# The softmax reciprocal of a windowed attention: 256 wide on VectorE, or four wide with a copy on GpSimd

## The chip, the cores and the metric

One core of one Trainium2 chip runs the whole program. The time is device microseconds of one execution, and the figure of a kernel is the median of its runs. The engines are named as the profile names them: PE is TensorE's matmul queue and PEld its weight loads, DVE is VectorE, ACT is ScalarE, POOL is GpSimd and SP issues the DMAs.

## The reference, cut to what matters

The program is one inference step of a two-layer decoder trunk: a pooling layer, then a layer of sliding-window attention, each followed by a convolutional feed-forward block and a gate. Prompt rows (1024) and sampled rows (8 sequences of 4) pass together. The change touches the attention of the prompt rows:

```python
s = einsum('nbqhgd,nbjhd->nbhgqj', q, k) * (HEAD_DIM ** -0.5)
s = where(valid, s + bias, -inf)
m = maximum(max(s, axis=-1, keepdims=True), sink)
e = exp(s - m)
p = e / (sum(e, axis=-1, keepdims=True) + exp(sink - m))
o = einsum('nbhgqj,nbjhd->nbqhgd', p, v)
```

There are 16 query heads of 64 values in four groups of four, one K/V head for each group, blocks of 128 queries, and 256 keys (the block before and the block itself) for each.

## The kernel before, in words

The matmul stages around the attention are one long stream of products in which each fp32 operand is split into a high and a low part (`xh` and `xl` for the activations, `wh` and `wl` for the weights, helper `split`, L140 and L141; products at L157 and L163 to L165). The attention stands in the middle, at about 1.1 to 1.33 ms.

The attention's work is cut into 32 items `(p, t, r)`: `p` is a pair of K/V heads (2), `t` a block of 128 queries (8), `r` one head of the pair (2). An item has four query heads, its index `g` within the tiles. Two items with the same `p` and `t` make a pair, which share an output bank. For an item, in order:

- `prep` (L919 to L930) splits the queries: the high half `qs` by ACT (r = 1, L925) or DVE (r = 0, L927), a copy of it into the other half by POOL (L928), and the low part `qz` by POOL (L929).
- `scores` (L932 to L949), in two halves of two heads: PE multiplies into one of two PSUM banks (L944, L945), and DVE adds the bias and takes the row maximum (L948).
- `peak` (L954, DVE) makes the negative maximum for the exponent, and `rest` (L958, DVE) the exponent of the sink.
- `exps` (L964 and L966, ACT) takes the exponentials; each gives its row sum into `sm[:, 2, g]`.
- `sums` (L970, DVE) adds the sink's term to the four sums.
- `flips` (L976, DVE) takes the reciprocals into the tile `rc`. It reads the four sums through a broadcast over 64 columns and so divides 128 x 256 elements; the 64 equal columns of a head are what the later transpose needs.
- `turn` (L988 to L991), for each half of the keys: PE transposes the exponentials into PSUM, ACT copies them out as the high part (L990), and DVE takes the low part (L991).
- `values` (L1011 to L1013, PE) multiplies them with V into the pair's output bank.
- For a pair: `spread` transposes `rc` (L998, PE) and copies it out (L1000, ACT), `scale` multiplies the output with it (L1017, DVE), and `outs` splits the result into `xh` (L1022, ACT) and `xl` (L1023, POOL).

Items 0 and 1 are begun inside the stream of the query projection, by the helpers `lead` and `soft`, where a planner orders the instructions. From item 2 on the order on every compute engine is the order written out in the loop at L1194 to L1221, under a manual schedule. One step of that loop, for `i`, works on several items at once: sums of item i + 2, `prep` of i + 5, scores of i + 4, exponentials of i + 3, transposes of i + 1, values of i, and at its end `flips` of i + 2 and `rest` of i + 4:

```python
at(i + 2, 2, sums)
at(i + 5, 6, prep)
...
pair(i, spread)
...
at(i + 2, 2, flips)
at(i + 4, 0, rest)
```

The reciprocals of an item are thus taken two steps before `spread` reads them. `rc` has three buffers, `sm` eight. At steps 0 to 8 of each half `p`, the attention of the sampled rows is put in between (`of_sample`), with a small reciprocal of its own at L1073. After the loop comes the output projection (L1286 to L1314), whose weights come by SP's queue into buffers that the attention held.

Of the kernel before, what the change touches and what calls it, by code (L numbers as in the profile page):

```python
# [21 lines left out]
P = 128  # L22
# [64 lines left out]
def trunk(ctx, tc, a, o):  # L87
    nc = tc.nc
    V, A, G, PE = nc.vector, nc.scalar, nc.gpsimd, nc.tensor
# [664 lines left out]
    def attention(es, awp, wv, E, rst):  # L754
# [162 lines left out]
        made = {}  # L917
# [54 lines left out]
        def flips(p, t, r):  # L972
            sm = made[p, t, r][1]
            if r == 0:
                made["rc", p, t] = ap_.tile([P, 4, 2, 64], F32, name="rc", tag="rc", bufs=3)
            V.reciprocal(out=made["rc", p, t][:, :, r, :], in_=sm[:, 2, :].unsqueeze(2).to_broadcast([P, 4, 64]))  # L976

        def turn(p, t, r, kt):

# [145 lines left out]
        def soft(it):  # L1125
            for gp in range(2):
                exps(*it, gp)
            sums(*it)
            flips(*it)
# [42 lines left out]
        with tc.manual_schedule(engines=COMPUTE):  # L1172
# [21 lines left out]
            for i in range(len(items)):  # L1194
                if i == 0:
                    n = q_squares()
                at(i + 2, 2, sums)
                at(i + 5, 6, prep)
                pair(i - 1, scale)
                at(i + 1, 0, turn, 0)  # L1200
                at(i, 0, values, 0)
                at(i + 4, 0, scores, 0)
                at(i + 3, 4, exps, 0)
                at(i + 4, 0, scores, 1)
                at(i + 1, 0, turn, 1)
                pair(i - 1, outs)
                at(i + 4, 0, peak)
                at(i + 3, 4, exps, 1)
                at(i, 0, values, 1)
                pair(i, spread)  # L1210
                p, t, r = items[i]
                step = 2 * t + r - 2
                if step in of_sample:
                    of_sample[step](p)
                at(i + 2, 2, flips)
                at(i + 4, 0, rest)
                if i == 0:
                    squares_sum(*n)
                    root(*n)
                if i == 1:  # L1220
                    scaled(*n)  # L1221
# [150 lines left out]
```

## Time and profile before

| | us |
|---|---|
| median of 3 runs | 2334.55 |
| lowest and highest | 2329.47, 2336.28 |
| the profiled execution | 2332.21 |
| its span in the profile | 2330.4 |

The profiled execution lies 2.34 us under the median; 1.81 us of it lie outside the span. Over the span the profile gives, for each engine, the time in which an instruction of it ran (busy), and for a stretch the TensorE clock that was granted, 1.00 being full speed. The mean of the clock over the span is 0.988. The chain of waits follows the work that ended last back from step to step; its pieces are shorter than the instruction's own duration where the next one on the same engine overlaps it.

### The profile page before, as it was taken

The page shows a single profiled execution, that of the slowest core. Times are in us where ns is not written, and L with a number is a line of the kernel's source. Part 1 is how long each engine was busy: PE and PEld are TensorE (multiplying, and loading weights), DVE is VectorE, ACT ScalarE, POOL GpSimd, SP SyncE. Part 2 cuts the span into 40 slices and gives each one's busy share as a digit, 9 for nine tenths or more (in the row PEclk, how much of TensorE's full clock was granted, in tenths as well). Part 3 has the DMA queues.
Part 4 walks back from the last instruction along what each step waited for, and adds up shares of the span by engine and source line. Part 5 has one row for each costly group of instructions (what it writes and reads, how often), then busy time and mean ns, then how long its engine had stood idle before and what let it go on. Part 6 is the DMA issues. An engine that isn't in the chain of part 4 may idle for free.

```text
span 2330.4 us, 34347 instructions
## 1 busy us (share of the span) xinstructions
PE 2272.7 (98%) x14037; PEld 2219.8 (95%) x14037; DVE 1403.1 (60%) x2122; ACT 822.7 (35%) x1489; POOL 443.6 (19%) x552
## 2 busy tenths in 40 slices
PE   9999999999999999999978899999999999999999
PEld 8999999999999999999866799999999999999898
DVE  5755555555556477567799827645555545555943
ACT  6532222222222244446677615322222222222532
POOL 1420001100001123314445313111000110001300
PEclk7899999999999999999999999999999999999999
DMA  4152211111111122312111141211111111111221
GB/s 137 32 129 87 64 46 46 46 46 46 46 46 46 46 68 75 95 43 49 28 46 28 59 109 55 73 52 46 46 46 46 46 46 46 46 46 47 61 78 43
DMA packets 199264, 133.09 MB, mean 57 GB/s; under 512 B 36355, under 2 KB 183508, under 8 KB 198939
## 3 DMA queue, kind: packets, MB, share of 16 engines
q1 hardware_dynamic: 199107, 130.90, 19.5%
q8 instruction: 110, 1.80, 0.3%
q14 instruction: 47, 0.39, 0.1%
HBM read 117.62 MB, written 18.79 MB: 59 GB/s over the span
## 4 chain that ended last, share of the span: by engine, by line
PE 82%; DVE 13%; ACT 2%; DMA 1%; issue 1%; SPq 1%; POOL 0%; ACTq 0%; DVEq 0%; POOLq 0%
PE mm L157 64%; DVE xl L212 2%; PE ub L163 2%; PE ub L164 2%; PE ub L165 2%; DVE rc L976 2%; PE dps L320 2%; DVE e L948 2%; DVE wl L991 1%; PE qkp L163 1%; PE qkp L165 1%; PE qkp L164 1%; DVE h L634 1%; DVE wl L141 1%; PE aux L163 1%
## 5 line engine op out<-in xcount | busy, mean ns | idle before, releaser
L157 PE MATMUL mm<-xh,wh 128*128 128x352 f32 x2208 | 477.6, 325 | 1.3 <-DVE ext L566 1.3
L157 PE MATMUL mm<-xh,wl 128*128 128x352 f32 x2208 | 476.6, 323 | 0.0
L157 PE MATMUL mm<-xl,wh 128*128 128x352 f32 x2208 | 475.7, 324 | 0.0
L140 ACT ACTIVATE wh<-wr 128x1024 fp32r<-128x1024 f32 x166 | 175.8, 1060 | 740.7 <-PE mm L157 623.3
L157 PEld LDWEIGHTS mm<-xh,wl 128*128 128x128 f32 x2208 | 379.0, 188 | 0.4 <-DVE wl L141 0.2
L157 PEld LDWEIGHTS mm<-xh,wh 128*128 128x128 f32 x2208 | 376.0, 189 | 1.5 <-issue 1.5
L157 PEld LDWEIGHTS mm<-xl,wh 128*128 128x128 f32 x2208 | 374.8, 188 | 0.6 <-issue 0.6
L563 DVE TENSOR_TENSOR ext<-mm,R 128x704 f32<-128x704 f32 x88 | 78.5, 892 | 474.7 <-PE mm L157 466.5
L569 POOL COPY sto<-ext 128x2 f32<-128x2 f32 x88 | 103.7, 1179 | 970.7 <-DVE ext L565 970.7
L624 DVE TENSOR_TENSOR h<-mm,h 128x1056 f32<-128x1056 f32 x160 | 200.9, 1256 | 115.6 <-PE mm L157 115.1
L141 DVE TENSOR_TENSOR wl<-wr,wh 128x1024 fp32r<-128x1024 f32 x164 | 204.9, 1250 | 8.9 <-ACT wh L140 8.9
L157 PE MATMUL mm<-ah,wh 128*128 128x352 f32 x960 | 208.2, 325 | 0.0
L157 PE MATMUL mm<-al,wh 128*128 128x352 f32 x960 | 207.4, 324 | 0.0
L157 PE MATMUL mm<-ah,wl 128*128 128x352 f32 x960 | 206.0, 323 | 0.0
L157 PEld LDWEIGHTS mm<-ah,wl 128*128 128x128 f32 x960 | 163.7, 189 | 0.0
L157 PEld LDWEIGHTS mm<-al,wh 128*128 128x128 f32 x960 | 163.4, 188 | 0.0
L157 PEld LDWEIGHTS mm<-ah,wh 128*128 128x128 f32 x960 | 162.4, 188 | 0.3
L163 PE MATMUL ub<-xh,wh 128*128 128x352 f32 x432 | 142.1, 329 | 0.1
L165 PE MATMUL ub<-xh,wl 128*128 128x352 f32 x432 | 140.2, 325 | 0.0
L164 PE MATMUL ub<-xl,wh 128*128 128x352 f32 x432 | 139.2, 322 | 0.0
L221 POOL TENSOR_TENSOR acc<-acc,sq 128x352 f32<-128x352 f32 x84 | 93.4, 1114 | 197.0 <-ACT sq L220 194.6
L576 DVE SCALAR_TENSOR_TENSOR cg<-ext,cw,cg 128x1072 f32<-128x1072 f32 x88 | 117.4, 1335 | 16.3 <-ACT cg L574 14.9
(275 smaller groups left out, 3634.7 us busy)
## 6 DMA issues: line engine op xcount, KB each, us to landing
wr<-in_w_up_dram SPq DMA_DIRECT2D x88, 512.0 KB
wr<-in_w_down_dram SPq DMA_DIRECT2D x44, 512.0 KB
wr<-in_w_ple_gate_dram SPq DMA_DIRECT2D x16, 512.0 KB
hd<-h SPq DMA_DIRECT2D x8, 528.0 KB
h<-hd SPq DMA_DIRECT2D x8, 528.0 KB
xt<-in_x_prompt_dram SPq DMA_DIRECT2D x8, 512.0 KB
wr<-in_w_q_dram SPq DMA_DIRECT2D x16, 256.0 KB
wr<-in_w_o_dram SPq DMA_DIRECT2D x32, 128.0 KB
```

The costliest lines, as they stand in the source:

```text
L140: A.activation(out=wh, in_=flat, func=AF.Copy)
L141: (low or V).tensor_tensor(out=wl, in0=flat, in1=wh.bitcast(F32), op=ALU.subtract)
L157: PE.matmul(ps[:, c, :C], w[k], b[k][:, c * C:(c + 1) * C], start=st, stop=sp)
L163: PE.matmul(ps, wh[k], bh[k][:, cs], start=k == 0, stop=False)
L164: PE.matmul(ps, wh[k], bl[k][:, cs], start=False, stop=False)
L165: PE.matmul(ps, wl[k], bh[k][:, cs], start=False, stop=k == nk - 1)
L212: V.scalar_tensor_tensor(out=xl[:, m, cs], in0=hm, scalar=gains[:, gain, m:m + 1], in1=xh[:, m, cs].bitcast(F32), op0=ALU.mult, op1=ALU.su ...
L221: G.tensor_tensor(out=st["acc"][:, cs], in0=st["acc"][:, cs], in1=sq, op=ALU.add)
L563: V.tensor_tensor(out=e[:, 2:2 + 2 * C].rearrange("p (c n) -> p c n", n=C), in0=ps[:, 0:2, :C], in1=R[:, :2 * C].rearrange("p (c n) -> p c ...
L569: G.tensor_copy(out=sto[:, j, 0:2], in_=e[:, NP:NP + 2])
L576: V.scalar_tensor_tensor(out=c, in0=e[:, k:k + CO], scalar=cw[:, k, j:j + 1], in1=c, op0=ALU.mult, op1=ALU.add)
L624: V.tensor_tensor(out=three(f.h[:, m, :]), in0=ps[:, :, :C], in1=three(f.h[:, m, :]), op=ALU.add)
```

## The change

```diff
         def flips(p, t, r):
             sm = made[p, t, r][1]
             if r == 0:
                 made["rc", p, t] = ap_.tile([P, 4, 2, 64], F32, name="rc", tag="rc", bufs=3)
-            V.reciprocal(out=made["rc", p, t][:, :, r, :], in_=sm[:, 2, :].unsqueeze(2).to_broadcast([P, 4, 64]))
+            V.reciprocal(out=sm[:, 3, :], in_=sm[:, 2, :])
+            G.tensor_copy(out=made["rc", p, t][:, :, r, :], in_=sm[:, 3, :].unsqueeze(2).to_broadcast([P, 4, 64]))
```

VectorE (`V`) takes four reciprocals in each partition into the fourth row of `sm`, which nothing used; GpSimd (`G`) copies them into `rc` through the same broadcast over 64 columns. `flips` stands at the same place of the written order.

## Rows read from the trace of the kernel before

**Rows 1.** The page, parts 1 and 4: busy time per engine, chain by line.

```profile
...
PE 2272.7 (98%) x14037; PEld 2219.8 (95%) x14037; DVE 1403.1 (60%) x2122; ACT 822.7 (35%) x1489; POOL 443.6 (19%) x552
...
PE mm L157 64%; DVE xl L212 2%; PE ub L163 2%; PE ub L164 2%; PE ub L165 2%; DVE rc L976 2%; PE dps L320 2%; DVE e L948 2%; DVE wl L991 1%; PE qkp L163 1%; PE qkp L165 1%; PE qkp L164 1%; DVE h L634 1%; DVE wl L141 1%; PE aux L163 1%
...
```

**Rows 2.** Windows: us; busy of PE, PEld, DVE, ACT, POOL (instructions); clock; DMA.

```profile
...
1130.00:1155.00 25.00, 23.82 (x151) 23.29 (x151) 18.40 (x45) 17.58 (x48) 6.63 (x7) 1.00 0.08 22
1173.43:1184.99 11.56, 8.82 (x45) 7.50 (x43) 9.73 (x24) 7.80 (x22) 3.16 (x3) 0.78 0.01 2
1184.99:1320.20 135.21, 108.86 (x710) 87.01 (x710) 132.90 (x425) 107.85 (x352) 68.81 (x97) 0.97 0.12 40
1320.20:1328.74 8.54, 6.60 (x37) 5.17 (x38) 8.54 (x11) 6.55 (x14) 2.58 (x2) 1.00 0.00 1
...
```

**Rows 3.** Chain of waits in one steady pair of heads: start us, us, what.

```profile
...
1266.18 0.60 DVE rbs L1017
...
1269.42 1.66 DVE rc L976
...
1271.10 0.07 DVE sm L970
...
1276.73 0.60 DVE rbs L1017
```

**Rows 4.** Windows of L976 alone: us, VectorE busy, instructions.

```profile
...
1184.99:1320.20 135.21, 45.27 (x26) 0.97 0.12 40
...
```

**Rows 5.** Line L976, its own view: ns min/median/max, first and last start.

```profile
...
L976 DVE RECIPROCAL rc<-sm x32: 1733/1742/1754, 1135.3 to 1324.2; 128x256 f32<-128x256 f32 x32
...
```

**Rows 6.** Groups of VectorE, 1173.43 to 1328.74: busy us, mean ns, idle before.

```profile
...
L976 DVE RECIPROCAL rc<-sm 128x256 f32<-128x256 f32 x30 | 52.2, 1741 | 0.1
...
```

**Rows 7.** Line L1073, the small reciprocal in the sampled step.

```profile
...
L1073 DVE RECIPROCAL sms<-sms x2: 166/166/166, 1219.1 to 1300.8; 128x2 f32<-128x2 f32 x2
...
```

**Rows 8.** Groups of ScalarE, 1173.43 to 1328.74: busy us, mean ns, idle before, releaser.

```profile
...
L964 ACT ACTIVATE e<-e,sm 128x256 f32<-128x256 f32 x104 | 51.7, 498 | 10.2 <-DVE sm L954 10.1
L990 ACT ACTIVATE wh<-trp 128x512 fp32r<-128x512 f32 x58 | 33.8, 585 | 7.3 <-PE trp L988 6.9
...
L1022 ACT ACTIVATE xh<-rbs 128x512 fp32r<-128x512 f32 x15 | 9.4, 630 | 9.8 <-DVE rbs L1017 9.6
...
L859 ACT ACTIVATE e<-e 128x352 f32<-128x352 f32 x1 | 0.5, 498 | 4.8 <-DVE e L855 4.8
...
```

**Rows 9.** Groups of GpSimd, whole run.

```profile
...
L569 POOL COPY sto<-ext 128x2 f32<-128x2 f32 x88 | 103.7, 1179 | 970.7 <-DVE ext L565 970.7
...
L929 POOL TENSOR_TENSOR qz<-q,qs 64x512 fp32r<-64x512 f32 x32 | 41.2, 1288 | 34.2 <-DVE qs L927 22.3 <-ACT qs L925 5.6 <-PE trp L988 5.1
...
L928 POOL CAST qs<-q 64x512 fp32r<-64x512 f32 x32 | 22.1, 691 | 2.5 <-PE sps L945 0.6
L912 POOL TENSOR_TENSOR wr<-wr,gains 128x1024 f32<-128x1024 f32 x10 | 20.6, 2056 | 9.2 <-DMA wr<-in_w_q_dram 5.9 <-DVE z L729 3.2
...
L570 POOL COPY sto<-ext 128x16 f32<-128x16 f32 x88 | 18.1, 205 | 0.0
...
L544 POOL COPY sin<-sto 128x704 f32<-128x704 f32 x2 | 1.6, 824 | 48.2 <-DVE sto L543 48.2
...
```

**Rows 10.** Timeline of VectorE, 1262.3 to 1276.7: start us, us, what.

```profile
...
1263.43 1.00 DVE L954 SCALAR_TENSOR_TENSOR sm<-sm,nsink 128x4 f32<-128x4 f32 x1
...
```

**Rows 11.** Timeline of GpSimd, the same stretch.

```profile
...
1263.10 1.32 POOL L929 TENSOR_TENSOR qz<-q,qs 64x512 fp32r<-64x512 f32 x1
...
```

**Rows 12.** Line L970, its own view.

```profile
...
L970 DVE TENSOR_TENSOR sm<-sm x32: 102/146/819, 1134.7 to 1323.0; 128x4 f32<-128x4 f32 x32
...
```

**Rows 13.** Timeline, end of the stage and start of the output projection.

```profile
...
1311.28 23.00 SPq L97 DMA_DIRECT2D wr<-in_w_o_dram  x11
...
1325.19 1.05 ACT L140 ACTIVATE wh<-wr 128x1024 fp32r<-128x1024 f32 x1
...
```

**Rows 14.** DMA of 1300 to 1345, 40 slices of 1.125 us.

```profile
...
GB/s 0 0 0 0 0 0 0 0 0 22 0 118 182 166 0 0 0 0 0 0 0 0 0 7 0 0 0 96 142 228 164 214 280 364 368 391 379 402 413 421
...
```

## The prediction

> **What bounds the kernel now.** I read the page first: its busy shares and the shares of the chain of waits [rows 1]. Over the whole span PE is busy 98% and VectorE 60%, so a reader might stop there and give the edit nothing. The chain says otherwise: L976 is 2% of it, some 47 us, although only 32 short instructions stand on that line. So VectorE must be the pace somewhere, and the average hides where.
>
> The second view is busy time by stretch [rows 2]. From 1184.99 to 1320.20, the steady part of the attention, VectorE is busy 132.90 of 135.21 us, 98%; ScalarE 107.85 (80%), PE 108.86 (81%), GpSimd 68.81 (51%). The same holds in the last 8.54 us. In the lead-in (1173.43 to 1184.99) VectorE is the busiest too, with 9.73 of 11.56 us. In this stage the reader must look at VectorE alone.
>
> The third view is the chain in one steady pair of heads [rows 3]. From one L1017 to the next it takes 10.55 us, all of it VectorE. Two reciprocals of 1.66 us each lie in that, 31% of it. The rows show one of the two.
>
> **What is removed.** 30 of the 32 reciprocals lie in the stage, 26 in its steady part [rows 4 to 6]. The two others belong to items 0 and 1 and run near 1135 us, where PE is busy 23.82 of 25 us [rows 2]: PE covers them, and I give nothing for them. Were that cover gone, they would be worth 2 x 1.6 us.
>
> A reciprocal of 128 x 256 takes 1742 ns [rows 5], one of 128 x 2 takes 166 ns [rows 7]. Per element that is (1742 - 166) / 254 = 6.2 ns, so 128 x 4 takes 166 + 2 x 6.2 = 178 ns. On the chain an instruction counts 0.08 us less than its duration (1.66 against 1.74, because the next one overlaps its end), so the new one counts 0.10 us. Each call frees 1.56 us of VectorE: 30 x 1.56 = 46.8 us over the stage, 40.6 in the steady part, where VectorE's work falls from 132.9 to 92.3 us.
>
> **What then sets the pace.** 92.3 is less than ScalarE's 107.85 and PE's 108.86, so the gain can't be 46.8. PE's figure contains modelled ends of pipelined matmuls; ScalarE's doesn't, so I reckon by ScalarE. Over the three stretches it is busy 7.80 + 107.85 + 6.55 = 122.2 of 155.3 us, idle 33.1. Its groups name what ended the idle time [rows 8]: 10.2 us waiting for the maximum of L954, 9.8 for the scaled output of L1017, 4.8 once for L855, together 24.8 us for VectorE; and 7.3 for PE's transposes. With VectorE at 92.3 us, the first three should go and the last may stay, since PE is as loaded as ScalarE. That gives **24.8 us**. The bounds: all of the idle time, 33.1 us, above; below, the figures of the second rival.
>
> **What is added.** GpSimd gets 32 copies of 128 x 256. None stands in the trace, so I bound one [rows 9]. Its copies of 128 x 16 take 205 ns and of 128 x 704 take 824 ns: 0.90 ns per element, so 205 + 240 x 0.90 = 421 ns. The low end is 0.21 us. The high end is 2.06 us, from L912, a two-input operation with a broadcast operand on four times the elements; L569 shows that a copy which VectorE holds up can be recorded at 1.18 us for two elements. I take 0.42, since the copies of the same kind are the nearest rows, and L912 (2.0 ns per element) shows no surcharge for a broadcast against L929 (1288 ns for 512, 2.5 per element). GpSimd's load in the steady part becomes 68.8 + 26 x 0.42 = 79.7 us, far from 107.9: beside other work, at no cost to the end.
>
> The copy waits for the reciprocal at the end of a step of the loop. Behind it in GpSimd's queue stand L928 (0.69 us) and L929 (1.29) of the next `prep`, and PE waits for those with its scores, one step later. Copy and both take 2.4 us of a step that lasts 5.3 now and over 4.1 after (107.85 / 26). GpSimd was the one that waited so far (34.2 us before L929), so this should fit. `spread` needs the copy two steps later, over 8 us: covered. No DMA and no semaphore of SP is moved.
>
> **Can the copies hold VectorE?** One row says that GpSimd does: the small L954 took 1.00 us from 1263.43, until the moment at which L929 on GpSimd, begun at 1263.10, ended [rows 10, 11]. L970, also 128 x 4, takes between 102 and 819 ns [rows 12]. Right behind the reciprocal, VectorE has L958 and L970, so each copy may hold one of them for up to 0.42 us: 26 x 0.42 = 10.9, which makes VectorE 103.2 us, still under 107.85. My sum stays. The Trainium skill has a rule that speaks against the change here: in "SBUF — State Buffer", section "Who interferes with whom", a VectorE instruction with two SBUF inputs and a GpSimd instruction that reads SBUF exclude each other, and the second to issue waits for the whole of the first. The case of L954 and L929 agrees with it. By that rule every one of the copies could hold VectorE, which is the case with 103.2 us, and its consequence is my second rival.
>
> **What comes after.** The output projection needs its first weights. Their DMA was issued at 1311.28 and the traffic had ended by 1315.75, in the 14th slice, while the first use is at 1325.19 [rows 13, 14]: 9.4 us spare. If the stage loses all of its idle share of ScalarE (33.1 of 155.3, 21%) in the 13.9 us between issue and use as well, that takes 3.0 of them. So the weights are still early, PE's stream starts sooner by what the stage saves, and nothing behind it gives that back.
>
> **The sum.** The profiled execution took 2332.21 us, 2.34 below the median of the runs shown. 2332.2 - 24.8 = 2307.4; against the median it would be 2309.8. I say **2308**.
>
> **The rivals.**
> 1. The forecast: ScalarE, closely followed by PE, becomes the pace; about 25 us less. Chance 0.70.
> 2. Three engines within 15% of each other, coupled by few PSUM banks, and small VectorE operations held by the copies: no engine gets near full. The lead-in, where none dominates, had its busiest engine at 9.73 / 11.56 = 84%. ScalarE at 84% makes the steady part 107.85 / 0.84 = 128.4 us, 6.8 less than now; with some of the 2 x 1.56 us in the lead-in and as much at the end, 7 to 12 us are saved: 2323 or so. For it: the held L954, on whose result ScalarE waited 10.2 us already. Against: with VectorE as the pace the stage ran at 98%. Chance 0.17, three quarters of it still over 7 us.
> 3. More than forecast: PE's waits go too, ScalarE never idles: 33.1 us less, 2299. The full 46.8 (2285) would need ScalarE's busy time itself to shrink, for which no row speaks. Chance 0.05.
> 4. Slower: GpSimd becomes the pace of the steady part. 68.81 + 26 c exceeds 107.85 from c = 1.5 us and 135.21 from c = 2.55 us; a copy of 3 us gives 146.8, 11.6 longer, 2344. It decides only if a copy takes longer than the four times larger L912. Chance 0.04.
> 5. The reciprocal doesn't get shorter with its size: no change, 2332. L1073 speaks against it. Chance 0.04.
>
> **How the numbers follow.** A measurement of this kernel can tell about 0.3%, 7 us, from no change. Faster by more: 0.70 + 0.05 + 0.13 of rival 2 = 0.88. Within: 0.04 of rival 2 + 0.04 of rival 5 = 0.08. Slower: 0.04. The range begins at 2295, which is the 2299 of all idle time gone with 4 us for the spread of single runs (2329.47 to 2336.28), and ends at 2322, about the middle of rival 2.
>
> **What would show it.** In the changed kernel's profile L976 is 32 instructions of about 0.18 us, and a new GpSimd copy group has 32 of 0.4. The steady part takes 110 to 117 us, VectorE about 80 to 90% busy in it, ScalarE over 92%. ScalarE's waits for L954 and L1017 are nearly gone; what it waits for is PE's transposes. Longer L958 and L970 would be the holding by the copies, harmless while ScalarE is full. I am wrong if ScalarE still waits for L954 or PE for the scores' `qz`, if a copy takes over 1.5 us, or if PE's stream after the stage waits for weights.

## The result, and the profile after

The changed kernel takes 2301.22 us, the median of 4 runs (2297.09 to 2306.16), against 2332.01 for the kernel before on the same chip (4 runs, 2323.73 to 2336.28). The ratio is 0.9873, its 95% interval 0.9838 to 0.9908: 30.8 us less in the medians. I had said 2308, between 2295 and 2322, and faster with 0.88.

The page of the changed kernel, as [rows 1]:

```profile
span 2295.3 us, 34410 instructions
...
PE 2257.1 (98%) x14037; PEld 2209.3 (96%) x14037; DVE 1368.8 (60%) x2122; ACT 820.5 (36%) x1489; POOL 458.2 (20%) x584
...
PE 84%; DVE 8%; ACT 3%; DMA 1%; POOL 1%; issue 1%; SPq 0%; ACTq 0%; POOLq 0%; DVEq 0%
...
```

The chain of waits by engine in the kernel before:

```profile
...
PE 82%; DVE 13%; ACT 2%; DMA 1%; issue 1%; SPq 1%; POOL 0%; ACTq 0%; DVEq 0%; POOLq 0%
...
```

VectorE's share of the chain of waits has fallen from 13% to 8%, although its share of the span is the same 60%. The average over the span would have shown nothing.

The three stretches of [rows 2] between the same instructions, that is from the first reciprocal of the loop to the first product of the output projection (us; then busy us and instructions of PE, PEld, VectorE, ScalarE, GpSimd; clock; DMA):

```profile
...
1167.07:1175.25 8.18, 7.48 (x43) 6.21 (x42) 6.34 (x26) 7.24 (x22) 4.77 (x6) 0.86 0.01 3
1175.25:1287.80 112.55, 101.36 (x706) 84.01 (x707) 105.13 (x424) 105.94 (x352) 81.29 (x124) 1.00 0.15 48
1287.80:1294.65 6.85, 6.85 (x43) 5.41 (x42) 4.96 (x12) 6.55 (x17) 3.09 (x4) 1.00 0.00 1
...
```

The same two instructions bound the stage of the kernel before at 1173.35 and 1328.50, which gives its lead-in and its end as follows:

```profile
...
1173.35:1184.99 11.64, 8.90 (x45) 7.58 (x44) 9.81 (x26) 7.80 (x22) 3.16 (x3) 0.78 0.01 2
...
1320.19:1328.50 8.31, 6.36 (x36) 4.93 (x37) 8.31 (x12) 6.31 (x14) 2.58 (x2) 1.00 0.00 1
...
```

The lead-in takes 8.2 us in place of 11.6, the steady part 112.6 in place of 135.2, the end 6.9 in place of 8.3. The stage takes 127.6 in place of 155.1 us, 27.5 less. The granted clock was lower in the stage of the kernel before (0.78 in the lead-in, 0.97 in the steady part), but that can account for little: VectorE was busy for all but 2.3 us of the steady part and 1.8 of the lead-in, and the changed kernel's lead-in takes 8.2 us at 0.86 and, in the first experiment, at 1.00. In the steady part ScalarE is now busy 94% and VectorE 93%; GpSimd's load went from 68.8 to 81.3 us.

ScalarE's groups over the three stretches (busy us, mean ns, idle before them), to be laid beside [rows 8]:

```profile
...
L964 ACT ACTIVATE e<-e,sm 128x256 f32<-128x256 f32 x104 | 51.7, 500 | 1.2 <-DVE sm L954 0.8
L991 ACT ACTIVATE wh<-trp 128x512 fp32r<-128x512 f32 x58 | 33.9, 587 | 3.4 <-PE trp L989 3.0
...
L1023 ACT ACTIVATE xh<-rbs 128x512 fp32r<-128x512 f32 x15 | 9.3, 620 | 0.0
...
L859 ACT ACTIVATE e<-e 128x352 f32<-128x352 f32 x1 | 0.5, 498 | 3.4 <-DVE e L855 3.4
...
```

The wait for L954 fell from 10.1 to 0.8 us, the one for the scaled output from 9.6 to nothing, and the one for L855 from 4.8 to 3.4 (its larger part lies ahead of the stage in both kernels; 2.3 and 0.8 us lie in it). The wait for PE's transposes, which I had left standing, fell from 6.9 to 3.0. In all ScalarE is idle 127.6 - 119.7 = 7.9 us, against 33.1.

The chain of waits through one pair of heads in the middle, shown in its longer pieces, is now ScalarE's alone, where it was VectorE's in [rows 3]:

```profile
...
1241.07 0.63 ACT qs L925
...
1241.73 0.60 ACT wh L991
...
1242.35 1.09 ACT e L964 x4
1243.45 0.48 ACT wh L991
1243.92 0.52 ACT xh L1023
1244.45 0.99 ACT e L964 x4
...
1245.53 0.48 ACT wh L991
...
1249.10 0.63 ACT qs L925
```

From one L925 to the next (1241.07 to 1249.10) a pair takes 8.0 us, against 10.55. (The mean over the steady part is 8.66, against 10.40.) This pair is one of two among the thirteen of the steady part that look so. Added up over the whole steady part, the pieces of the chain are 37 us of PE, 34 of ScalarE, 20 of GpSimd and 12 of VectorE, where VectorE had 119 of 135 us in the kernel before. So one engine's hold on the stage has given way to several that take turns, and the experiments have to say what each of them is worth.

The two new operations, by the views of their lines (ns min/median/max, first and last start):

```profile
...
L976 DVE RECIPROCAL sm<-sm x32: 158/166/178, 1129.5 to 1291.9; 128x4 f32<-128x4 f32 x32
...
```

```profile
...
L977 POOL COPY rc<-sm x32: 395/400/672, 1129.7 to 1292.1; 128x256 f32<-128x256 f32 x32
...
```

The reciprocal takes 166 ns (I had worked out 178), the copy 400 (421), with a mean of 452 in the steady part, where some copies meet other work.

The profiled execution of the changed kernel took 2297.09 us, 35.1 less than the one of before. Only 27.5 of them lie in the stage; 6.3 lie ahead of it and 1.3 behind it. The granted clock of the first 57 us, in the changed kernel's window:

```profile
...
0.00:57.00 57.00, 51.35 (x315) 45.43 (x316) 40.74 (x89) 42.00 (x94) 11.62 (x18) 0.91 0.45 144
...
```

It is 0.91 there, a mean between the clock's two levels of 1.2 and 2.4 GHz. In the kernel before:

```profile
...
0.00:57.00 57.00, 52.17 (x269) 46.40 (x270) 32.23 (x74) 38.60 (x84) 9.89 (x16) 0.76 0.44 140
...
```

There it is 0.76. The first experiment shows that this belongs to the execution and not to the change.

### The profile page after: what moved, and what is told of

The parts are those of the page before. It is cut to its first block, busy times and chain, and to the rows that moved or that the text cites. A ratio compares the mean times of both kernels' runs of the same rounds, so it can differ in the third digit from the quotient of the medians.

```text
span 2295.3 us, 34410 instructions
## 1 busy us (share of the span) xinstructions
PE 2257.1 (98%) x14037; PEld 2209.3 (96%) x14037; DVE 1368.8 (60%) x2122; ACT 820.5 (36%) x1489; POOL 458.2 (20%) x584
## 4 chain that ended last, share of the span: by engine, by line
PE 84%; DVE 8%; ACT 3%; DMA 1%; POOL 1%; issue 1%; SPq 0%; ACTq 0%; POOLq 0%; DVEq 0%
PE mm L157 65%; DVE xl L212 2%; PE ub L163 2%; PE ub L164 2%; PE ub L165 2%; PE qkp L163 1%; PE qkp L165 1%; PE qkp L164 1%; PE dps L320 1%; DVE wl L141 1%; DVE h L634 1%; ACT e L964 1%; PE aux L163 1%; PE aux L165 1%; PE aux L164 1%
## 5 line engine op out<-in xcount | busy, mean ns | idle before, releaser
L140 ACT ACTIVATE wh<-wr 128x1024 fp32r<-128x1024 f32 x166 | 175.7, 1059 | 739.8 <-PE mm L157 623.4
L141 DVE TENSOR_TENSOR wl<-wr,wh 128x1024 fp32r<-128x1024 f32 x164 | 204.2, 1246 | 9.6 <-ACT wh L140 8.9
```

Of the source, the lines that this page charges most:

```text
L140: A.activation(out=wh, in_=flat, func=AF.Copy)
L141: (low or V).tensor_tensor(out=wl, in0=flat, in1=wh.bitcast(F32), op=ALU.subtract)
```

## The experiments

All experiments start from the changed kernel and are compared with the kernel before on their own chip. Since the ratios have intervals of about 0.4% in all, the reading goes by the steady part of the stage (from the end of the first scaled output to the end of the fourteenth), which took 112.55 and 112.58 us in two executions of the same kernel. The table has one traced execution of each version; under an engine's name stands its busy time in the steady part. Differences under one microsecond I leave alone. The granted clock of the steady part was 0.98 with the copy later and with two copies, 0.99 with the copy on VectorE and with the reciprocal 16 wide, and 1.00 in the other versions of the changed kernel; what it costs there is contained in their times.

| run | stage, us | steady part, us | VectorE | ScalarE | GpSimd | PE | ratio to before (95%) |
|---|---|---|---|---|---|---|---|
| before | 155.15 | 135.20 | 132.89 | 107.85 | 68.81 | 108.86 | |
| changed, once more | 127.60 | 112.58 | 105.23 | 105.98 | 81.25 | 101.29 | 0.9882 (0.9864 to 0.9900) |
| no copy | 130.39 | 112.16 | 104.02 | 105.78 | 70.18 | 106.60 | 0.9886 (0.9867 to 0.9906) |
| copy on VectorE | 137.35 | 121.29 | 115.27 | 106.97 | 69.25 | 104.28 | 0.9931 (0.9915 to 0.9947) |
| copy one step later | 127.99 | 112.55 | 105.06 | 105.37 | 79.36 | 102.66 | 0.9886 (0.9870 to 0.9902) |
| copy made twice | 130.17 | 113.58 | 106.54 | 105.72 | 91.90 | 100.63 | 0.9872 (0.9852 to 0.9891) |
| reciprocal 16 wide | 129.54 | 113.91 | 109.40 | 106.15 | 81.38 | 102.80 | 0.9868 (0.9853 to 0.9884) |
| more ScalarE | 135.46 | 119.60 | 106.47 | 113.77 | 81.11 | 104.98 | 0.9909 (0.9894 to 0.9924) |
| query split on GpSimd | 126.13 | 109.85 | 106.62 | 97.35 | 89.72 | 100.03 | 0.9873 (0.9856 to 0.9889) |
| the same, copy later | 124.21 | 107.92 | 105.43 | 96.57 | 85.80 | 98.77 | 0.9875 (0.9854 to 0.9897) |
| query split on VectorE | 125.39 | 109.81 | 105.40 | 97.01 | 81.98 | 100.10 | 0.9861 (0.9844 to 0.9877) |

**The changed kernel once more**, with no edit.

> The changed kernel once more, as the scale for the others on the same chip. Theory (ScalarE sets the pace of the attention stage now, with PE close behind): 28 to 32 us under the kernel before, and a stage (first reciprocal of the loop to the first product of the output projection) of about 129 us against 155 before. If part of the first result was the lower clock with which that execution of the kernel before began (granted clock 0.76 in its first 57 us against 0.91), the stage still takes 129 and the whole gain comes out nearer to 26.

Measured: 2301.54 us against 2328.39, 26.9 less. That is under the 28 to 32 and near the 26 of the other case. Its windows:

```profile
...
1171.63:1179.80 8.17, 6.09 (x41) 4.95 (x39) 6.33 (x26) 7.22 (x21) 4.75 (x6) 1.00 0.01 3
1179.80:1292.38 112.58, 101.29 (x706) 83.93 (x707) 105.23 (x424) 105.98 (x353) 81.25 (x124) 1.00 0.15 48
1292.38:1299.23 6.85, 6.85 (x43) 5.41 (x42) 4.98 (x12) 6.56 (x17) 3.11 (x4) 1.00 0.00 1
...
```

This execution began as the one of before did:

```profile
...
0.00:57.00 57.00, 52.17 (x269) 46.31 (x270) 32.28 (x74) 38.67 (x84) 9.95 (x16) 0.76 0.42 140
...
```

With 0.76 again, the loop starts 1.7 us before that of the kernel before, not 6.3. The steady part repeats to 0.03 us. So the gain of the change is that of the stage, 27.5 us, and most of the rest of the 35.1 us between the first two profiles came with the execution. Comparing PE's instructions one by one, in order, shows where what is left arises: 1.25 of the 1.7 us between 147 and 153 us, long before the attention, 0.45 between 1149 and 1154 us, just ahead of the loop, and 1.6 between 2185 and 2193 us, long after it. The last two are there in both executions of the changed kernel; no run shows their cause.

**ScalarE's work raised.** The copy of the transposed reciprocals is made twice.

```diff
             A.activation(out=made["rb"].rearrange("p g n -> p (g n)"), in_=rb, func=AF.Copy)
+            A.activation(out=made["rb"].rearrange("p g n -> p (g n)"), in_=rb, func=AF.Copy)
```

> ScalarE's copy of the transposed reciprocals is made twice: 14 x 0.58 = 8.1 us more ScalarE in the steady part (112.6 us), nothing else. Theory (ScalarE is the pace there): the steady part takes 118 to 121 us. Rival (VectorE or PE is as much the pace, and ScalarE has room): under 115 us.

```profile
...
1181.91:1301.51 119.60, 104.98 (x710) 84.13 (x709) 106.47 (x425) 113.77 (x366) 81.11 (x124) 1.00 0.14 45
...
```

7.8 us more ScalarE (113.77 against 105.98) make the steady part 7.0 us longer (119.60), within what the theory said and out of the rival's reach. The second copy stands between PE's transposes and the scaled output, but that output waited for it only once, for 0.3 us; so it is ScalarE's time that counts. Added work on ScalarE is paid nearly in full, and in this sense ScalarE is the pace of the changed kernel there, though the chain runs through the other engines too.

**VectorE's work raised.** The reciprocal is taken 16 wide.

```diff
-            V.reciprocal(out=sm[:, 3, :], in_=sm[:, 2, :])
-            G.tensor_copy(out=made["rc", p, t][:, :, r, :], in_=sm[:, 3, :].unsqueeze(2).to_broadcast([P, 4, 64]))
+            if r == 0:
+                made["half", p, t] = ap_.tile([P, 2, 4, 16], F32, name="rh", tag="rh", bufs=3)
+            V.reciprocal(out=made["half", p, t][:, r], in_=sm[:, 2, :].unsqueeze(2).to_broadcast([P, 4, 16]))
+            G.tensor_copy(out=made["rc", p, t][:, :, r, :], in_=made["half", p, t][:, r, :, 0:1].to_broadcast([P, 4, 64]))
```

> The reciprocal is taken of 16 equal columns for each sum, 128 x 64, by the two measured sizes about 0.55 us in place of 0.17: 26 x 0.385 = 10.0 us more VectorE in the steady part, GpSimd's copy unchanged. Theory (ScalarE paces, VectorE has some 7 us of room): 3 to 5 us longer than 112.6. Rival (VectorE is as much the pace as before the change): 8 to 10 us longer.

VectorE's groups in the steady part (busy us, mean ns):

```profile
...
L978 DVE RECIPROCAL rh<-sm 128x64 f32<-128x64 f32 x26 | 14.1, 541 | 0.1
...
L958 DVE TENSOR_TENSOR sm<-sm,nsink 128x4 f32<-128x4 f32 x26 | 3.8, 147 | 0.0
...
```

The reciprocals take 14.1 us, 9.8 more than the 4.3 of the changed kernel, and the steady part is only 1.3 us longer, less than either theory said. VectorE's busy time rose by 4.2, not by 9.8: L958 fell from 8.2 to 3.8 us. Part of what the profile calls busy in VectorE was waiting for GpSimd inside small instructions (the run without a copy, below, shows how), and it gave way. So narrowing the reciprocal to a quarter, from 256 to 64 elements, already brings all of the gain in the steady part but 1.3 us (in the stage, 1.9).

**No copy.** PE reads the four reciprocals through a broadcast as its weights.

```diff
-            if r == 0:
-                made["rc", p, t] = ap_.tile([P, 4, 2, 64], F32, name="rc", tag="rc", bufs=3)
             V.reciprocal(out=sm[:, 3, :], in_=sm[:, 2, :])
-            G.tensor_copy(out=made["rc", p, t][:, :, r, :], in_=sm[:, 3, :].unsqueeze(2).to_broadcast([P, 4, 64]))
...
-            rc = made.pop(("rc", p, t)).rearrange("p g r d -> p g (r d)")
             for g in range(4):
-                PE.transpose(rb[:, g * P:(g + 1) * P], rc[:, g, :], ident)
+                for r in range(2):
+                    PE.matmul(rb[half[r], g * P:(g + 1) * P], made[p, t, r][1][:, 3, g:g + 1].to_broadcast([P, 64]), ident, start=True, stop=True)
```

> No copy at all: PE reads the four reciprocals through a broadcast as its weights, with 8 small matmuls for a pair in place of 4. Theory (ScalarE paces, the copy lies beside): VectorE's small operations L954 and L958 shrink from 12.3 and 8.6 us to about 8 and 3, VectorE's busy time in the steady part falls by about 11 us, and the stage gets only 0 to 3 us shorter than 129, since ScalarE had 7.9 us idle in all. Rival (GpSimd's queue and the held VectorE operations are on the path): 5 us or more shorter.

The steady part takes 112.16 us: without the copies nothing is gained there. The edit isn't free of cost, though: PE is busy 5.3 us longer in the steady part, and this run alone can't tell whether that hides a gain. The stage as a whole came out longer, 130.4 us against 127.6, in the lead-in and the end, where PE has no lead: its part for the reciprocals takes 1.0 us for a pair there and took 0.44. That miss is the edit's own. The three small VectorE operations, without any copy:

```profile
...
L954 DVE SCALAR_TENSOR_TENSOR sm<-sm,nsink 128x4 f32<-128x4 f32 x26 | 12.7, 489 | 0.0
...
L958 DVE TENSOR_TENSOR sm<-sm,nsink 128x4 f32<-128x4 f32 x26 | 6.3, 243 | 0.0
L970 DVE TENSOR_TENSOR sm<-sm 128x4 f32<-128x4 f32 x26 | 5.4, 209 | 0.0
...
```

and in the changed kernel:

```profile
...
L954 DVE SCALAR_TENSOR_TENSOR sm<-sm,nsink 128x4 f32<-128x4 f32 x26 | 12.0, 462 | 0.0
...
L958 DVE TENSOR_TENSOR sm<-sm,nsink 128x4 f32<-128x4 f32 x26 | 8.2, 316 | 0.0
...
L970 DVE TENSOR_TENSOR sm<-sm 128x4 f32<-128x4 f32 x26 | 4.0, 156 | 0.0
...
```

In the kernel before:

```profile
...
L954 DVE SCALAR_TENSOR_TENSOR sm<-sm,nsink 128x4 f32<-128x4 f32 x26 | 7.5, 288 | 0.0
...
L970 DVE TENSOR_TENSOR sm<-sm 128x4 f32<-128x4 f32 x26 | 3.8, 145 | 0.0
L958 DVE TENSOR_TENSOR sm<-sm,nsink 128x4 f32<-128x4 f32 x26 | 2.4, 94 | 0.0
...
```

The three sum to 24.4 us without a copy, 24.2 in the changed kernel and 13.7 in the kernel before. So they are held longer than before, but not by the copies, as I had it, and VectorE's busy time did not fall by the 11 us that I expected (104.0 against 105.2). One case of the changed kernel, in the timelines of VectorE and GpSimd:

```profile
...
1244.94 0.96 DVE L954 SCALAR_TENSOR_TENSOR sm<-sm,nsink 128x4 f32<-128x4 f32 x1
1245.82 0.16 DVE L976 RECIPROCAL sm<-sm 128x4 f32<-128x4 f32 x1
...
```

```profile
...
1241.85 0.61 POOL L928 CAST qs<-q 64x512 fp32r<-64x512 f32 x1
...
1244.59 1.29 POOL L1024 TENSOR_TENSOR xl<-rbs,xh 128x512 fp32r<-128x512 f32 x1 [0.75 <-ACT xh L1023]
...
```

L954 began at 1244.94 and ended at 1245.90, when L1024 on GpSimd (begun 1244.59) had ended at 1245.88. In this case it is an older, longer operation of GpSimd that holds it. The others are alike: of these 78 small operations in the steady part of the changed kernel, 16 take over 200 ns, and every one of them ends 15 to 23 ns after an operation of GpSimd that began before it. In 12 cases that is L1024, in two L929 and in two L1041 (a copy for the sampled rows); in none is it the new copy. What the new copies do hold is L927, VectorE's part of the query split: four of its twelve start behind a copy and take 619 to 639 ns, where all twelve take 408 to 414 in the kernel before and without a copy. In all L927 takes 1.4 us more.

**The copy on VectorE.**

```diff
-            G.tensor_copy(out=made["rc", p, t][:, :, r, :], in_=sm[:, 3, :].unsqueeze(2).to_broadcast([P, 4, 64]))
+            V.tensor_copy(out=made["rc", p, t][:, :, r, :], in_=sm[:, 3, :].unsqueeze(2).to_broadcast([P, 4, 64]))
```

> The copy on VectorE in place of GpSimd: about 0.3 us more on VectorE for each of 30 copies, 9 us in the stage, against about 11 us of holding that goes. Theory (ScalarE paces): the stage stays within 2 us of 129. Rival (GpSimd's copy costs on the path): 4 us or more shorter.

Both were wrong: the steady part is 8.7 us longer (121.29), VectorE is busy 115.3 us in it, more than the changed kernel's steady part lasts, and the ratio, 0.9931, lies outside the interval of the changed kernel on the same chip. The copy's line, by its own view:

```profile
...
L977 DVE COPY rc<-sm x32: 293/296/1398, 1135.3 to 1305.4; 128x256 f32<-128x256 f32 x32
...
```

Its median is 296 ns, but the 26 of the steady part take 14.2 us, 545 ns each. One of them, and what GpSimd did then:

```profile
...
1245.81 1.18 DVE L977 COPY rc<-sm 128x256 f32<-128x256 f32 x1
...
```

```profile
...
1245.56 1.28 POOL L1024 TENSOR_TENSOR xl<-rbs,xh 128x512 fp32r<-128x512 f32 x1 [0.89 <-ACT xh L1023]
...
```

The copy took 1.18 us from 1245.81 and ended 0.15 us after L1024. So it is with all 11 of the 26 copies that take over 300 ns (504 to 1398): each ends 0.15 us after an operation of GpSimd that began before it. By the Trainium skill, "SBUF — State Buffer", section "Who interferes with whom", a copy on VectorE can run in a mode that takes the port which it shares with GpSimd, and the second to issue waits for the first. The rows agree. So GpSimd as the place of the copy is worth 8.7 of the 22.6 us that the steady part gained.

**The copy made twice, and one step later.** The first repeats the line of the copy; the second makes that line a helper of its own, `widen`, and puts it behind the next step's query split (the call in the loop is shown):

```diff
                 at(i + 5, 6, prep)
+                at(i + 1, 2, widen)
                 pair(i - 1, scale)
```

> GpSimd makes its copy of the reciprocals twice: 26 x 0.4 = 10.4 us more GpSimd in the steady part (81 to 92 us of 112.6). Theory (the copy lies beside other work, as leaving it out showed): within 2 us of 112.6. Rival (GpSimd's queue is on the path): 4 us longer or more.

> The copy stays on GpSimd but stands one step later, behind the query split of that step (L928 and L929 as the changed kernel numbers them), so that these no longer wait behind it for the reciprocal. If the copy's place in GpSimd's queue is what makes PE wait for the query's low part (4.3 us of PE, 6.8 us of its weight loads), these waits nearly go and the stage is 3 to 5 us shorter. Theory (ScalarE paces): at most 2 us shorter.

Twice the copy costs 1.0 us in the steady part (113.58) and 2.6 in the stage, for 10.7 us more GpSimd in the steady part: GpSimd has room. One step later costs and brings nothing (112.55), although PE's wait for the query's low part was halved. That wait had grown with the change. In the kernel before, where L944 has a part of it:

```profile
...
L944 PE MATMUL sps<-kx,qs 128*128 128x256 f32 x100 | 29.8, 321 | 6.1 <-DVE sm L948 4.4 <-POOL qz L929 1.4
L945 PE MATMUL sps<-kx,qz 128*128 128x256 f32 x100 | 27.0, 295 | 0.3 <-POOL qz L929 0.3
...
```

in the changed kernel:

```profile
...
L945 PE MATMUL sps<-kx,qz 128*128 128x256 f32 x100 | 26.4, 294 | 4.5 <-POOL qz L929 4.3
...
```

and with the copy later:

```profile
...
L945 PE MATMUL sps<-kx,qz 128*128 128x256 f32 x100 | 26.1, 291 | 2.3 <-POOL qz L929 2.0
...
```

PE's 2.3 us less of that wait did not shorten the stage, so the wait as a whole was not what bounded it. A gain of about a microsecond isn't excluded: at the clock of 0.98 PE is busy 1.4 us longer in this run.

**ScalarE relieved.** The high half of the queries for r = 1 (L925) goes to GpSimd; then the same together with the copy one step later; then to VectorE.

```diff
-                A.activation(out=qs[own], in_=q4, func=AF.Copy)
+                G.tensor_copy(out=qs[own], in_=q4)
```

> The high half of the queries (L925, for r = 1) goes from ScalarE to GpSimd: 13 x 0.63 = 8.2 us less ScalarE, as much more on GpSimd (81 to 89 of 112.6 us). Theory (ScalarE paces, VectorE with 105 us next): the steady part takes 105 to 109 us, the kernel some 5 us less than the changed one. Rival (VectorE, held by GpSimd's operations, paces or GpSimd's queue is late with the query's low part): no shorter, or longer.

> Two edits together: the high half of the queries for r = 1 on GpSimd in place of ScalarE (which alone took the steady part to 109.9 us, with PE 6.9 us idle for the query's low part), and the copy of the reciprocals one step later in GpSimd's queue (which alone changed nothing, while PE's wait for the low part fell from 4.3 to 2.0 us). If GpSimd's queue holds PE up once ScalarE is relieved, the steady part takes 106 to 109 us. If VectorE (106.6 of 109.9 us busy) is the next pace, it stays at 109 to 111.

> The high half of the queries for r = 1 on VectorE in place of ScalarE: 8.2 us less ScalarE (98 in the steady part), 13 x 0.41 = 5.3 us more VectorE. VectorE took 10 us more with 1.3 us of effect when ScalarE was the pace; with ScalarE at 98 us it is VectorE that paces: 109 to 113 us in the steady part, no clear gain over 112.6. Rival (VectorE's busy time is mostly holding that gives way): 105 to 108 us.

On GpSimd the steady part takes 109.85 us, 2.7 less for 8.6 us less ScalarE, which is less than I had expected and more than the rival allowed. With the copy later it takes 107.92, as expected if GpSimd's queue holds PE up once ScalarE is relieved. On VectorE it takes 109.81, within the range expected, but 2.8 us shorter than the changed kernel where I had expected no clear gain. The shortest:

```profile
...
1177.17:1285.09 107.92, 98.77 (x706) 83.78 (x707) 105.43 (x425) 96.57 (x338) 85.80 (x135) 1.00 0.15 50
...
```

VectorE is then busy 98%. The steady part gets up to 4.7 us shorter by this and the stage 3.4, under 0.2% of the kernel. The intervals of all three ratios overlap that of the changed kernel, so no version here beats it by what can be measured.

## Why the prediction was right

- **What bounded the kernel** was right: VectorE in the attention, seen by stretch and not over the span. Taking work from VectorE gave 27.5 us in the stage; putting 9.8 us back cost 1.3, while 7.8 us more ScalarE cost 7.0.
- **What is removed** was right in size: 1.58 us of duration for each reciprocal (1742 to 166 ns). The gain is less than the 46.8 us of it, for the reason given: ScalarE, and PE close behind it, then limit the stage. The forecast had VectorE far below them, at 92.3 us in the steady part; it is at 105.1, so that three engines lie within 5 us of each other (PE 101.4, ScalarE 105.9).
- **The gain of 24.8 us**, ScalarE's waits for VectorE, was 27.5 in the stage, and the nearness is partly luck. The wait for L855 was read as 4.8 us, but only 2.3 of them lie in the stage, so the three waits held 22.4. Of these 20.8 went. The transposes, which I let stand, gave 3.8, and a wait of L140 for PE's products 1.0. The last 2.2 us came from no wait: the durations of ScalarE's instructions sum to the same as before (151.7 and 152.1 us), but packed more closely they overlap more, and its busy time fell from 122.0 to 119.7. The term that I sized too low is PE's transposes. Some of PE's lateness was VectorE's, one step removed: in PE's queue the transposes stand behind the products with the low part, and these waited for VectorE in the kernel before (this link is read from the order of the queue and not tested):

```profile
...
L1013 PE MATMUL ops<-wl,vh 128*128 128x512 f32 x59 | 25.8, 437 | 12.9 <-DVE wl L991 12.6
...
```

and in the changed kernel:

```profile
...
L1014 PE MATMUL ops<-wl,vh 128*128 128x512 f32 x59 | 23.9, 404 | 0.9 <-DVE wl L992 0.9
...
```

- **The copy** costs nothing that can be measured on GpSimd: right. Making it twice cost 1.0 us in the steady part, and neither leaving it out nor putting it later gained anything. Its 421 ns were 400, or 452 on average in the steady part.
- **The copies hold VectorE for up to 10.9 us**: the size came out by luck, since the cause was another. VectorE's busy time came to 105 us, near the 103.2 of that case and over my 80 to 90%, but it does so without any copy too. The three small operations take 10.5 us more than in the kernel before, and it is older operations of GpSimd that hold them; the copies hold four operations of L927, and L927 takes 1.4 us more in all.
- **One of my signs of being wrong did show**: PE waits for the scores' `qz`, 4.3 us against 1.7 in the kernel before. Halving this wait gained nothing while ScalarE was as loaded as it is (112.55), and 1.9 us once ScalarE was relieved (109.85 to 107.92). It is a limit close behind the others, not the one that decided.
- **The weights of the projection** are still early: PE keeps its lead over the kernel before to within 0.2 us from the end of the stage to 1361 us, and no wait for their DMA shows between 1287 and 1345 us.
- **The time**, 2308, was 6.8 us too high: 2.7 by the stage, and the rest lies outside it and is no more than single runs of the changed kernel lie apart (2297.09 to 2306.16).

## What to carry to other kernels

A broadcast operand on a slow elementwise operation computes the same value many times; compute it once and repeat it with an engine that has room. Find the stretch in which the slow engine is the pace, and estimate the gain by the idle time that the next engine spends waiting for it, not by the work removed. That is no bound: waits that the profile lays to a third engine can go too, as here (22.4 us estimated so, 27.5 gained, out of 33.1 idle). When the idle time is nearly gone, more savings on the first engine bring little: here narrowing the operation to a quarter brought all of the 22.6 us of the steady part but 1.3.

## What was not expected of the hardware

A copy of 128 x 256 fp32 takes VectorE 296 ns by itself and 400 ns on GpSimd, and yet it costs less on GpSimd: beside GpSimd's other work VectorE needed 545 ns for one on average, and up to 1398. Nor is VectorE's busy time on small instructions all work: L958 alone shrank by 4.4 us in the steady part when the reciprocal ahead of it got longer, since it then met GpSimd at other moments: two of its 26 operations were held by one of GpSimd's, in place of six. A VectorE instruction of 128 x 4 can so pay nearly the whole length of a GpSimd operation that began just before it (1246 ns against 1287), and the profile shows it as busy.
